# Attention scores on halves of TensorE's rows, and branch outputs split by quarters, in a hybrid decoder layer

## The chip, the core and the metric

The kernel runs on one core of a Trainium2 chip. The metric is the device time of one execution, in microseconds (us); a lower time is better. Before the change the median of three runs is 769.07 us (769.01 to 769.11). In the profile PE is TensorE (PEld its weight loads), DVE is VectorE, ACT is ScalarE, POOL is GpSimd and SP is SyncE.

## The reference, cut to what matters

One layer over 512 tokens of width 1024, in float32. Three branches of attention read the same normalized input: a sliding-window one (8 query heads and 2 key heads of 64, band of two blocks of 128 keys), a stick-breaking one (8 heads of 64) and one over a memory of 256 tokens. Their outputs go through one matrix each, are gated and summed; then come an output matrix, a norm, and a SwiGLU feed-forward.

```
u = rms_norm(h, ln_mix_pre[l])
proj = jnp.einsum('bsd,de->bse', u, w_in[l])
qa, ka, va, qb, kb, vb, qm, gl = jnp.split(proj, split_idx, axis=-1)
# sliding window, per head of 64 and block of 128 queries
scores = jnp.einsum('bnqhgd,bnkhd->bnhgqk', qb, kband) * (d ** -0.5)
...
# stick-breaking, per head of 64: a[t,s] = beta_ts * prod over s<j<t of (1 - beta_tj)
z = jnp.einsum('bqhd,bkhd->bhqk', q[:, i * BLOCK:L], k[:, :L]) * (d ** -0.5)
...
merged = (g[:, :, 0] * jnp.einsum('bse,ed->bsd', y_swa, w_branch_swa[l])
          + g[:, :, 1] * jnp.einsum('bse,ed->bsd', y_sb, w_branch_sb[l])
          + g[:, :, 2] * jnp.einsum('bse,ed->bsd', y_mem, w_branch_mem[l]))
mix = jnp.einsum('bsd,de->bse', merged, w_out[l])
```

## The kernel before, in words

**Products.** A float32 factor is split into a high part in a short float format (fp32r) and the low part that is left over. `split` (L423) does it: ACT casts the high part, DVE subtracts. `parts` (L548) makes two buffers of it. `mm3` (L455) then multiplies with three matmuls, high by high, high by low, and low by high. Nearly all of PE's stream consists of such threes, with 128 rows of weights and 256 or 512 columns of data. The large products (gates, branch matrices, feed-forward) are made in a form with seven products of quarters p1 to p7 in place of eight.

**Stages.** The head loads the first weights and x, sums the squares of x on PE with a matrix of ones (`rstd_of`, L518; its two matmuls use the high and the low part sh_x and sl_x, and on_x holds the ones), and begins the first three key projections (L1141 to L1209; nine matmuls on a constant run before them). `proj` (L581) makes the projections of queries and keys, transposed: 128 rows are the 64 dimensions of two heads, c = 0 to 3 counts such pairs. Then come the stick-breaking heads, the sliding-window heads and the memory heads, with projections, gates and branch products run between as a stream of weights (`dn.run(us)`), then the output matrix and the feed-forward.

**Scores before.** A head has 64 dimensions, and its three products are put into two matmuls over all 128 rows: `stack_parts` (L553) builds, for each head, a buffer with the high part in one half of the rows and the low part in the other (kbs for stick-breaking keys, qas for sliding-window queries). `stack_twice` (L564) builds a buffer with the high part in both halves (qbs, kas) and one with the low part in one half and zeros in the other (qbl, kal). `sb_head` (L1273) has these two matmuls for each of four blocks of queries (keys 512, 384, 256 and 256 columns wide), and three PSUM banks for a head:

```
mm(out, qs[:, q], keys, r < 3, False)
mm(out, ql[:, q], keys, False, r != 2)
```

Then come two sigmoids for each bank, the mask and a scan along the row, `sb_turn` (L1306) turns the weights by transposes, and `sb_out` (L1323) sums the values for two heads at once, each head on one half of TensorE's columns (at and wide in the profile). `swa_pair` (L1348) has four blocks of 256 keys for each of two heads, two matmuls each, later a softmax, transposes, and weighted sums on halves of the columns (pts and wide).

**Branch outputs before.** `pair_out` (L1265) takes a bank with the outputs of two heads: it splits it from the bank into a high and a low buffer, and `seven_raw` (L892) copies the bank once more, in quarters, from which the sums for p3, p5, p6, p7 are made. p1, p2 and p4 use the split parts directly (`seven_left`, L913).

**Order.** Engines run their instructions in the order in which they were given. Tables of numbers (`ORDER`, one for each engine, L38 to L147) fix that order and `follow` (L480) ties each instruction to the one ahead. `PLAN` (L148 to L179) gives each tile its buffer: eight PSUM banks, four raw, high and low weight buffers, and single and paired buffers of 512 columns (ck, pair). All instructions go through a helper that records them, so that the profile gives line L232 for every one; names of tiles tell them apart.

Of the kernel before, what the change touches and what calls it, by code (L numbers as in the profile page):

```python
# [37 lines left out]
ORDER = {  # L38
    "tensor": (
# [23 lines left out]
    ),  # L63
    "vector": (
# [81 lines left out]
    ),  # L146
}  # L147
PLAN = {  # L148
    "raw": (
# [2042 lines left out]
```

## Time and profile before

| | before |
|---|---|
| median of three runs | 769.07 us |
| span of the profiled execution | 766.9 us |
| PE busy | 759.1 us (99%), 4073 matmuls |
| DVE busy | 675.2 us (88%), 1100 instructions |
| ACT busy | 520.3 us (68%), 946 instructions |
| POOL busy | 104.1 us (14%) |
| last matmul ends, from the span's start | 760.3 us |

The profiled execution's span runs from its first to its last instruction; the median of the runs is 2.2 us above it. Busy times of engines overlap. In the timeline a row has its start, its duration, the engine, the operation, output tile, inputs, and their shapes (`128*128` is the part of TensorE's array that is used: rows by columns); equal instructions in a run stand in one row with their count. The end of a matmul is modelled, and the next starts before it, so starts are compared. In brackets stands how long the engine idled just before, and for what. A group has busy time and the mean of one in ns.

### The profile page before, as it was taken

To read this page: it belongs to the slowest core of one execution; us is meant where nothing else is said; L and a number is where in the kernel's file an instruction comes from. 1 tells how busy PE (TensorE), PEld (TensorE's weight loads), DVE (VectorE), ACT (ScalarE), POOL (GpSimd) and SP (SyncE) were. 2 spreads that over 40 slices of the span, in tenths; PEclk is the share of its full clock that TensorE was granted. 3 is DMA by queue.
4 is the path that set the end of the run, shared out by engine and by line. 5 is a ranking of instruction groups with operands and counts; after the bars stand their busy time and mean duration, and the time that the engine had idled before them with its cause. 6 is when DMAs were issued, how large, how long until landed. Compare 5 with 4: busy or idle time off the path is not lost.

```text
span 766.9 us, 11497 instructions
## 1 busy us (share of the span) xinstructions
PE 759.1 (99%) x4073; PEld 647.3 (84%) x4073; DVE 675.2 (88%) x1100; ACT 520.3 (68%) x946; POOL 104.1 (14%) x140
## 2 busy tenths in 40 slices
PE   9999999999999999999999999999999999999996
PEld 6789888778888888888888899988888888888885
DVE  7994897799989756999897799899999999999966
ACT  7662677777997758677944596566666668957552
POOL 0303242000222110010001201100000000214000
PEclk9999999999999999999999999999999999999998
DMA  8548999734799895469949958876777746859922
GB/s 277 166 142 233 332 328 254 211 111 149 185 188 192 184 203 163 112 134 210 340 128 329 209 130 240 203 191 180 204 192 203 220 142 187 171 120 216 261 75 111
DMA packets 50170, 150.06 MB, mean 196 GB/s; under 512 B 5984, under 2 KB 7952, under 8 KB 50016
## 3 DMA queue, kind: packets, MB, share of 16 engines
q1 hardware_dynamic: 34224, 94.38, 36.8%
q0 software_dynamic: 15600, 54.80, 36.1%
q8 instruction: 32, 0.52, 0.3%
q14 instruction: 26, 0.21, 0.1%
q10 hardware_dynamic: 288, 0.13, 0.1%
HBM read 140.38 MB, written 19.40 MB: 208 GB/s over the span
## 4 chain that ended last, share of the span: by engine, by line
PE 96%; DMA 1%; DVE 1%; ACT 1%; issue 0%; SPq 0%; DVEq 0%
PE bank L232 96%; DMA xT<-in_xT 1%; DMA raw<-in_w_p 0%; DVE xacc L232 0%; SPq L232 0%; ACT pair L232 0%; DVE pair L232 0%; ACT hi L232 0%; ACT xT L232 0%; DVE lo L232 0%; DVE fg L232 0%; DVE sl_x L232 0%; DVEq L2180 0%; DVE s L232 0%; ACT sqr L232 0%
## 5 line engine op out<-in xcount | busy, mean ns | idle before, releaser
L232 PE MATMUL bank<-pair,hi 128*128 128x512 f32 (+1 forms) x1008 | 254.4, 368 | 0.0
L232 DVE TENSOR_TENSOR lo<-raw,hi 128x1024 fp32r<-128x1024 f32 (+4 forms) x149 | 170.7, 1149 | 36.8 <-ACT hi L232 36.2
L232 PEld LDWEIGHTS bank<-pair,hi 128*128 128x128 f32 x1008 | 177.5, 189 | 27.0 <-ACT hi L232 0.9
L232 ACT CAST hi<-raw 128x1024 fp32r<-128x1024 f32 (+4 forms) x149 | 147.7, 998 | 73.7 <-PE bank L232 54.5
L232 PE MATMUL bank<-hi,pair 128*128 128x512 f32 (+1 forms) x628 | 196.3, 374 | 0.0
L232 PE MATMUL bank<-pair,lo 128*128 128x256 f32 (+1 forms) x752 | 154.7, 302 | 0.0
L232 PEld LDWEIGHTS bank<-hi,pair 128*128 128x128 f32 x628 | 115.3, 188 | 19.5 <-issue 0.2
L232 PEld LDWEIGHTS bank<-pair,lo 128*128 128x128 f32 x752 | 115.6, 190 | 10.9 <-DVE lo L232 0.7
L232 PE MATMUL bank<-lo,pair 128*128 128x512 f32 (+1 forms) x330 | 123.6, 375 | 0.0
L232 ACT CAST hi<-wide 128x1024 fp32r<-128x1024 f32 (+1 forms) x61 | 62.2, 1024 | 27.0 <-PE bank L232 11.3
L232 DVE TENSOR_TENSOR lo<-wide,hi 128x1024 fp32r<-128x1024 f32 (+1 forms) x61 | 71.9, 1185 | 4.6 <-ACT hi L232 4.3
L232 PEld LDWEIGHTS bank<-lo,pair 128*128 128x128 f32 x330 | 62.0, 188 | 10.1
L232 POOL DMA_DIRECT2D raw<-in_w_g x24 | 21.1, 878 | 124.4 <-DVE lo L232 106.2
L232 DVE TENSOR_TENSOR gp<-gp,bank 128x512 f32<-128x512 f32 x49 | 33.6, 687 | 4.6 <-PE bank L232 3.7
L232 ACT ACTIVATE sg<-gp 128x256 f32<-128x256 f32 x42 | 17.7, 421 | 23.0 <-DVE gp L232 22.9
L232 POOL DMA_DIRECT2D raw<-in_w_gu x15 | 13.2, 924 | 147.6 <-DMA raw<-in_w_gu 138.5
L232 ACT COPY gp<-bank 128x512 f32<-128x512 f32 x42 | 24.7, 588 | 2.1 <-DVE aq L232 1.4
L232 DVE TENSOR_TENSOR_SCAN bw<-br,bw 128x512 f32<-128x512 f32 (+3 forms) x32 | 24.6, 809 | 0.2
L232 DVE TENSOR_TENSOR gp<-gp,hp 128x512 f32<-128x512 f32 x36 | 24.7, 685 | 0.0
L232 POOL DMA_DIRECT2D wide<-in_w_gu x12 | 11.2, 934 | 84.6 <-DMA wide<-in_w_gu 76.3
L232 ACT COPY hp<-bank 128x512 f32<-128x512 f32 x36 | 21.5, 598 | 0.0
L232 PE MATMUL bank<-hi,ll 128*128 128x512 f32 x50 | 19.4, 389 | 0.0
(624 smaller groups left out, 1371.8 us busy)
## 6 DMA issues: line engine op xcount, KB each, us to landing
wide<-in_w_gu SPq DMA_DIRECT2D x31, 512.0 KB, 5.1
raw<-in_w_gu SPq DMA_DIRECT2D x26, 512.0 KB, 5.4
raw<-in_w_g POOLq DMA_DIRECT2D x24, 512.0 KB, 6.0
raw<-in_w_g SPq DMA_DIRECT2D x18, 512.0 KB, 4.2
raw<-in_w_gu POOLq DMA_DIRECT2D x15, 512.0 KB, 7.2
raw<-in_w_p SPq DMA_DIRECT2D x14, 512.0 KB, 6.3
wide<-in_w_gu POOLq DMA_DIRECT2D x12, 512.0 KB, 5.8
raw<-in_w_brt SPq DMA_DIRECT2D x9, 512.0 KB, 4.8
```

The lines of the kernel that those rows point to most:

```text
L232: ins = f(*args, **kw)
```

## The change

1. Queries and keys of both branches are split by plain `parts` on all 128 rows: one cast and one subtraction of 128x512 for a pair of heads. `stack_parts`, `stack_twice` and the zeroed halves go.
2. Scores come from a new function. It makes the three products on 64 rows, once for rows 0 to 63 (the first head of the pair) and once for rows 64 to 127 (the second head), into different banks, head by head in turn. There are 192 score matmuls in place of 128. Two stick-breaking heads start together and hold six banks; `sb_head` becomes `sb_scores`, `sb_weights` and `sb_turn`, and the loop goes over pairs.

```
-        ks, qs, ql = (st[(x, c, h % 2)] for x in ("kbs", "qbs", "qbl"))
...
-            mm(out, qs[:, q], keys, r < 3, False)
-            mm(out, ql[:, q], keys, False, r != 2)
+    def mm3_rows(outs, l, r, start):
+        for x, y_ in ((0, 0), (1, 0), (0, 1)):
+            for e, out in enumerate(outs):
+                rows = slice(64 * e, 64 * e + 64)
+                mm(out, l[x][rows], r[y_][rows], start and x + y_ == 0, y_ == 1)
+    def sb_scores(c):
+        (kh, kl), (qh, ql) = st[("kbs", c)], st[("qbs", c)]
+        z = [[aps(f"z{2 * c + e}{i}") for i in range(3)] for e in range(2)]
...
+            mm3_rows([z[e][i][:, o : o + n] for e in range(2)], (qh[:, q], ql[:, q]), keys, r < 3)
+        for e in range(2):
+            sb_weights(2 * c + e, z[e])
...
-    for h in range(8):
-        sb_head(h)
...
+    sb_scores(0)
+    dn.run(5.6)
+    for c in range(4):
+        sb_turn(2 * c)
...
+        if c < 3:
+            sb_scores(c + 1)
+        dn.run(3.0)
+        sb_turn(2 * c + 1)
```

3. A branch output leaves its bank once, in the quarters' copies. The quarters that are left factors of p1, p2 and p4 are split from those copies: three splits for a branch, where it was four from the bank.

```
+    YRAW = dict(p1=(0, 0), p2=(1, 0), p4=(1, 1))
...
     def pair_out(b, c, ps):
-        y[(b, c)] = parts(f"y{b}{c}", ps)
-        if b in SEVENS:
-            seven_raw(b, c, ps)
...
+        for p, quarter_of in YRAW.items():
+            if c % 2 == 1 and quarter_of[0] == c // 2:
+                ysum[(b, p)] = parts(f"ys{b}{p}", yq[(b, *quarter_of)])
```

4. Instructions are no longer issued while the program is built. They are noted (`Program`, `Notes`, `View`) and put out at the end in one global order, from which each engine's order follows; unused other paths are dropped. The profile's line becomes L421 (`put_out`). `ORDER` and `PLAN` have new numbers throughout, of which this line tells nothing more than that:

```
+    "2826 2829 2702 2827 2844 2830-2831 2711 2832-2833 2820 2845 3143 2834 2846-2849 2723 2850 2855 2838 2856 "
```

Counted over the program: matmuls 4009 before and 4073 after (the profile's page of before counts 64 more than the program has), ACT casts and copies 581 and 565, ACT table loads 9 and 10 (the new one ahead of the first logarithm), DVE two-tensor operations 761 and 745, DVE copies 20 and 10, POOL's zeroings 17 and 7. A stretch of PE's order in which the array is used in one form (whole, by halves of the columns, by halves of the rows) is followed by one in another form: there are 17 stretches before (8 of them halves of the columns) and 35 after (8 halves of the columns, 13 halves of the rows, 14 whole). Before, each column stretch lies between two stretches of the whole array; after, the order goes directly between row halves and column halves eight times.

In the new order PE's first stick-breaking scores, which stood before as these rows (kbs keys, qbs and pair the two query buffers, hi and lo weights):

```order
L232 MATMUL bank_104<-kbs_316,qbs_409 128x512
L232 MATMUL bank_104<-kbs_316,pair_111 128x512
L232 MATMUL bank_104<-kbs_316,qbs_409 128x384
L232 MATMUL bank_104<-kbs_316,pair_111 128x384
L232 MATMUL bank_104<-kbs_316,qbs_409 128x256
L232 MATMUL bank_104<-kbs_316,pair_111 128x256
```

now stand as these (a last letter h or l is the high or the low part, x2 the two halves of the rows):

```order
L421 MATMUL bank_101<-kbs0h,qbs0h 128x384 x2
L421 MATMUL bank_101<-kbs0h,qbs0l 128x384 x2
L421 MATMUL bank_101<-kbs0l,qbs0h 128x384 x2
L421 MATMUL bank_101<-kbs0h,qbs0h 128x512 x2
L421 MATMUL bank_101<-kbs0h,qbs0l 128x512 x2
L421 MATMUL bank_101<-kbs0l,qbs0h 128x512 x2
L421 MATMUL bank_101<-kbs0h,qbs0h 128x256 x2
```

Every block of queries has three such pairs for two heads, in place of two matmuls for each head.

On PE the two matmuls of the sum of squares stood next to each other (they are the rows with on_x):

```order
L232 MATMUL bank_104<-pair_109,lo_82 128x512
L232 MATMUL bank_104<-sh_x,on_x 128x512
L232 MATMUL bank_104<-sl_x,on_x 128x512
L232 MATMUL bank_104<-pair_111,hi_79 128x512
L232 MATMUL bank_104<-pair_114,hi_79 128x512
```

Now, with pair_102 the ones and pair_112 and pair_113 the high and the low part of the sum, they are apart:

```order
L421 MATMUL bank_101<-pair_112,pair_102 128x512
L421 MATMUL bank_101<-pair_104,hi_79 128x512
L421 MATMUL bank_101<-pair_105,hi_79 128x512
L421 MATMUL bank_101<-pair_104,lo_83 128x512
L421 MATMUL bank_101<-pair_105,hi_79 128x512
L421 MATMUL bank_101<-pair_106,hi_79 128x512
L421 MATMUL bank_101<-pair_105,lo_83 128x512
L421 MATMUL bank_101<-pair_106,hi_79 128x512
L421 MATMUL bank_101<-pair_113,pair_102 128x512
```

Seven matmuls of the fourth projection have moved between them.

At the head of DVE's order stood these (pair and wide are the first block of u and of x, lo_80 the low part of the first weight):

```order
L232 CAST on_x<-const-bfloat16-1.0 128x128
L232 CAST on_m<-const-bfloat16-1.0 128x128
L232 MEMSET none 1x512
L232 MEMSET eps_t 128x1
L232 TENSOR_SCALAR pair_111<-wide_84 128x256
L232 SCALAR_TENSOR_TENSOR pair_114<-wide_84,pair_111 128x512
L232 TENSOR_TENSOR lo_80<-raw_72,hi_76 128x128
```

Now they stand so (pair_102 is on_x, the first pair_104 takes the place of on_m):

```order
L421 CAST pair_102<-const-bfloat16-1.0 128x128
L421 TENSOR_TENSOR lo_80<-raw_72,hi_76 128x128
L421 CAST pair_104<-const-bfloat16-1.0 128x128
L421 TENSOR_SCALAR pair_104<-wide_84 128x256
L421 MEMSET eps_t 128x1
L421 SCALAR_TENSOR_TENSOR pair_105<-wide_84,pair_104 128x512
```

The low part of the first weight and a cast of ones have moved ahead of the first block of u.

More of the change, by code (lines that the diff above doesn't have):

```diff
@@ L1 @@
 import math
-from contextlib import ExitStack, nullcontext
+from contextlib import ExitStack
 import numpy as np
@@ new lines, with __init__, then, __getitem__ @@
+class View:
+    def __init__(self, make, path=(), shape=None):
+        self.make, self.path, self.shape = make, path, shape
+    def then(self, f):
+        return View(self.make, self.path + (f,))
+    def __getitem__(self, k):
+        return self.then(lambda ap: ap[k])
+    def bitcast(self, dt):
+        return self.then(lambda ap: ap.bitcast(dt))
+    def rearrange(self, *args, **kw):
+        return self.then(lambda ap: ap.rearrange(*args, **kw))
+    def unsqueeze(self, axis):
+        return self.then(lambda ap: ap.unsqueeze(axis))
+    def to_broadcast(self, shape):
+        return self.then(lambda ap: ap.to_broadcast(shape))
+    def real(self):
+        ap = self.make()
+        for f in self.path:
+            ap = f(ap)
+        return ap
@@ new lines, with __init__, put_out @@
+class Op:
+    def __init__(self, at, engine, name, args, kw):
+        self.at, self.engine, self.name, self.args, self.kw = at, engine, name, args, kw
+        self.behind = ()
+class Program:
+    def __init__(self):
+        self.ops = []
+    def put_out(self, nc, order, follow):
+        real = lambda x: x.real() if isinstance(x, View) else x
+        last, out = {}, set()
+        for n in order or range(len(self.ops)):
+            op = self.ops[n]
+            assert all(b.at in out for b in op.behind)
+            out.add(n)
+            args = [real(x) for x in op.args]
+            ins = getattr(getattr(nc, op.engine), op.name)(*args, **{k: real(x) for k, x in op.kw.items()})
+            if op.engine in last:
+                follow(ins, last[op.engine])
+            last[op.engine] = ins
+        assert len(out) == len(self.ops)
@@ L256, in __getitem__, with once, f @@
         return self.held[c]
+def once(make):
+    got = []
+    def f():
+        if not got:
+            got.append(make())
+        return got[0]
+    return f
 class Places:
@@ L268, in open, with fixed, take @@
     def open(self, pool, kind, n, shape, dt=F32):
[L269 removed]
+        for i in range(n):
             key = f"{kind}{i}"
             self.held[key] = pool.tile(shape, dt, tag=key, name=key, bufs=1)
[L273 to L277 removed]
+    def fixed(self, shape, name):
         if name == "v_all":
             self.spare = self.used
[L280 to L287 removed]
+        t = self.held["wide0"][:, self.used : self.used + shape[1]]
+        self.used += shape[1]
+        return t
+    def take(self, pool, kind, shape, dt, name):
         n = int(next(self.plan[kind]))
         if kind == "ck" and n < SINGLES:
[L290 removed]
+            return View(once(lambda: pool.tile(shape, dt, tag=f"ck{n}", name=name, bufs=1)))
         if kind == "ck":
+            assert dt == F32R
             n -= SINGLES
@@ L380, in tile_kernel @@
 def tile_kernel(ctx, tc, a):
-    nc = Core(tc.nc)
+    program = Program()
+    nc = Core(program)
     places = Places()
@@ L425, in split @@
         ins = nc.scalar.copy(hi, raw)
-        lows = nc.vector.tensor_tensor(lo, raw, hi.bitcast(F32), op=ALU.subtract)
-        if "behind" in st:
-            after(ins, st["behind"][0])
-            after(lows, st["behind"][1])
+        nc.vector.tensor_tensor(lo, raw, hi.bitcast(F32), op=ALU.subtract)
         return ins
@@ L441, in w_split @@
         uid[0] += 1
-        hi = places.take(wp, "hi", [P, 1024], F32R, f"hi{uid[0]}", bufs=4)
-        lo = places.take(wp, "lo", [P, 1024], F32R, f"lo{uid[0]}", bufs=4)
+        hi = places.take(wp, "hi", [P, 1024], F32R, f"hi{uid[0]}")
+        lo = places.take(wp, "lo", [P, 1024], F32R, f"lo{uid[0]}")
         if isinstance(raw, list):
             for i, x in enumerate(raw):
-                ins = split(x[:, :], hi[:, i * 512 : (i + 1) * 512], lo[:, i * 512 : (i + 1) * 512])
+                split(x[:, :], hi[:, i * 512 : (i + 1) * 512], lo[:, i * 512 : (i + 1) * 512])
         else:
-            ins = split(raw[:, :n], hi[:, :n], lo[:, :n])
-        if "chain" in st:
-            after(ins, st["chain"])
+            split(raw[:, :n], hi[:, :n], lo[:, :n])
         return hi, lo
@@ L456, in mm3 @@
         (lh, ll), (rh, rl) = l, r
-        one = nc.tensor.matmul(out, lh, rh, start=start, stop=False, skip_group_check=True)
+        nc.tensor.matmul(out, lh, rh, start=start, stop=False, skip_group_check=True)
         nc.tensor.matmul(out, lh, rl, start=False, stop=False, skip_group_check=True)
-        return one, nc.tensor.matmul(out, ll, rh, start=False, stop=stop, skip_group_check=True)
-    def mm3_behind(*args):
-        one, last = mm3(*args)
-        if "products" in st:
-            after(one, st["products"])
-        st["products"] = last
+        nc.tensor.matmul(out, ll, rh, start=False, stop=stop, skip_group_check=True)
     def mm(out, l, r, start, stop):
@@ L474, in tile_kernel @@
     pin, since = [], []
-    def after(ins, first):
-        if not ORDER:
-            follow(ins, first)
     def follow(ins, first):
@@ L486, in fn @@
         ins = nc.scalar.activation(*args, **kw)
-        for p in pin:
-            after(ins, p)
+        ins.behind = tuple(pin)
         since.append(ins)
@@ L494, in table, with const @@
         ins = nc.scalar.preload_act_table_set(name)
-        for x in since:
-            after(ins, x)
+        ins.behind = tuple(since)
         since.clear()
         pin[:] = [ins]
-    def const(name, shape, pool=cst):
-        t = places.fixed(cst, shape, F32, f"c_{name}") if pool is cst else pool.tile(shape, F32, name=f"c_{name}")
+    def const(name, shape, pool=None):
+        t = pool.tile(shape, F32, name=f"c_{name}") if pool else places.fixed(shape, f"c_{name}")
         nc.sync.dma_start(t[:, :], a[name])
@@ L1210, in tile_kernel @@
-    pin[:] = [first_table]
+    idle = tc.nc.const_aps.tensor(1.0, [P, 512], BF16)
+    one_t = {}
+    for name in ("x", "m"):
+        one_t[name] = ck(f"on_{name}", F32R)[:, :P]
+        nc.vector.tensor_copy(one_t[name], idle[:, :P])
+    pw = dps("warm")
+    for i in range(WARM):
+        mm(pw[:, :], idle[:, :P], idle[:, :], True, True)
+    first_load(nc.scalar, 0, (0, 2))
+    first_table = nc.scalar.preload_act_table_set("natural_log_exp_and_others")
+    pin[:] = [first_table]
+    load_x(0, 1)
@@ new lines, in tile_kernel @@
+    first_load(nc.sync, 0, (1,))
+    load_x(1, 2)
+    first_load(nc.sync, 1, (0, 1))
+    load_x(2, 3)
+    first_load(nc.sync, 1, (2,))
+    first_load(nc.sync, 2, (0,))
+    load_x(3, 4)
+    first_load(nc.sync, 2, (1, 2))
+    load_x(4, 5)
+    first_load(nc.sync, 3)
+    load_x(5, 8)
+    dn.loaded = dn.have = FIRST
+    for p in range(len(PIECE)):
+        for i in range(FIRST):
+            first_split(i, p)
+        for k in range(*PIECE[p]):
+            gain_split(k)
+    xacc = ck("xacc")
@@ new lines, in tile_kernel @@
+    nc.scalar.activation(xacc[:, :], xraw[0][:, :], AF.Square)
+    for k in range(1, KC):
+        nc.scalar.activation(xraw[k][:, :], xraw[k][:, :], AF.Square)
+        nc.vector.tensor_tensor(xacc[:, :], xacc[:, :], xraw[k][:, :], op=ALU.add)
+    dn.ahead(4, 3)
+    for i in range(FIRST):
+        first_ps[("kb", i)] = aps(f"kb{i}")
+    order = [(i, 0, x) for x in ("hh", "lh", "hl") for i in range(FIRST)]
+    order += [(i, 1, x) for i in range(FIRST) for x in ("hh", "lh", "hl")]
+    for i, k, x in order:
+        w = (his if x[0] == "h" else los)[i]
+        mm(first_ps[("kb", i)][:, :], w[:, k * P : (k + 1) * P], u[k][x[1] == "l"], k == 0 and x == "hh", False)
@@ L1212, in tile_kernel @@
+    gens = [dn.units[i]["mm"](his[i], los[i]) for i in range(FIRST)]
+    for k in range(2, KC + 1):
+        for g in gens:
+            next(g, None)
+    dn.at = FIRST
+    st["rs"], st["rb"] = rstd_of("x", xacc, S, aps)
+    for f in st.pop("waiting"):
+        f()
     ident = const("ident", [P, P], base)
-    sinks = places.fixed(cst, [P, 8], F32, "sinks")
+    sinks = places.fixed([P, 8], "sinks")
     nc.sync.dma_start(sinks[:, :], a["sinks"].to_broadcast([P, 8]))
@@ L1620, in turn @@
         st[("t1", t)] = t1
-        return place("T1", t, t1)
+        place("T1", t, t1)
     def kept(t):
@@ L2065, in tile_kernel @@
     kept(1)
-    behind(since[-1], st["mixed"])
     table("silu_and_others")
@@ L2071, in tile_kernel @@
     go(3)
-    behind(*turn(3, tmp[3]))
+    turn(3, tmp[3])
     fs.hold = 5
@@ L2075, in tile_kernel @@
     turn_n2(2)
-    behind(*turn_n2(3))
+    turn_n2(3)
     fs.hold = 6
@@ L2079, in tile_kernel @@
     turn_n22(2)
-    behind(*turn_n22(3))
+    turn_n22(3)
     fs.hold = 8
@@ L2089, in tile_kernel @@
         turn_late(t, 1)
-    st.pop("behind")
     fs.hold = 10**6
@@ L2094, in tile_kernel @@
     go(len(fs.units))
-    for e, text in ORDER.items():
-        seen, last = getattr(nc, e).seen, None
-        for part in text.split():
-            a, _, b = part.partition("-")
-            for k in range(int(a), int(b or a) + 1):
-                if last is not None:
-                    follow(seen[k], seen[last])
-                last = k
+    order = []
+    for part in ORDER.split():
+        a, _, b = part.partition("-")
+        order += range(int(a), int(b or a) + 1)
+    program.put_out(tc.nc, order, follow)
 def _buckets():
```

411 lines of the change are left out of this document (118 added, 293 removed), and 421 rows, old and new, of tables (ORDER, PLAN).

## The prediction

> **What bounds the kernel now.** I began with the page's head and its table of busy time.
>
> ```profile
> span 766.9 us, 11497 instructions
> PE 759.1 (99%) x4073; PEld 647.3 (84%) x4073; DVE 675.2 (88%) x1100; ACT 520.3 (68%) x946; POOL 104.1 (14%) x140
> ```
>
> TensorE (PE) is busy for 99% of the span, VectorE (DVE) for 88%. A busy PE may still be waiting inside, so the waits of PE came next, and the chain that ended last.
>
> ```profile
> PE bank L232 <- PEq L2174: 0.8, 1, 0.8
> PE bank L232 <- DVE sl_x L232: 0.4, 1, 0.4
> ```
>
> ```profile
> 22.29 737.97 PE bank L232 x3990
> ```
>
> PE waits twice: 0.8 us at the start, and 0.4 us for one low part (sl_x). From 22.29 us the chain is PE alone, 3990 matmuls to 760.3 us. The table by stretches gives the two ends (first column the stretch, then its length, busy time of PE, PEld, DVE, ACT, POOL; granted clock third from the end).
>
> ```profile
> 4.75:80.00 75.25, 74.88 (x396) 66.10 (x396) 61.40 (x100) 44.09 (x73) 15.59 (x29) 1.00 0.69 210
> ...
> 760.30:766.93 6.63, 0.00 (x0) 0.00 (x0) 2.46 (x6) 1.17 (x4) 0.00 (x0) 0.68 0.43 158
> ```
>
> The clock is full from the first real matmul, so a gain or a loss will have to be a change in PE's stream: matmul time, gaps at a change of form, waits. The last 6.6 us (final sums, output) follow PE's end, and the change leaves their work as it is: 0.
>
> Work taken off DVE and ACT is worth nothing by itself. The groups show what such work is: the halves of heads were split by instructions like this one.
>
> ```profile
> L232 DVE TENSOR_TENSOR kbs<-kb,kbs 64x512 fp32r<-64x512 f32 x5 | 3.4, 685 | 0.1
> L232 ACT ACT_TABLE_LOAD x9 | 11.5, 1283 | 1.8 <-PEq L2174 1.7
> ```
>
> DVE issues 16 subtractions fewer, about 16 x 0.685 = 11 us, and 10 small copies. But PE waited for DVE 0.4 us in all, so at most that could come back, and it is counted below in its place. ACT gets a table load more, 1.28 us, ahead of the first logarithm; the projections that fill the banks meanwhile cover it, and if that cover is gone it costs 1.28 us.
>
> **1. The scores.** In the timeline of the first stick-breaking head (start, duration; a row's end is modelled, so I count from start to start):
>
> ```profile
> 81.53 0.40 PE L232 MATMUL bank<-kbs,qbs 128*128 128x512 f32 x1
> 81.76 0.39 PE L232 MATMUL bank<-kbs,pair 128*128 128x512 f32 x1
> 81.99 0.33 PE L232 MATMUL bank<-kbs,qbs 128*128 128x384 f32 x1
> 82.16 0.34 PE L232 MATMUL bank<-kbs,pair 128*128 128x384 f32 x1
> 82.33 0.28 PE L232 MATMUL bank<-kbs,qbs 128*128 128x256 f32 x1
> 82.45 0.28 PE L232 MATMUL bank<-kbs,pair 128*128 128x256 f32 x1
> ...
> 82.82 0.40 PE L232 MATMUL bank<-pair,hi 128*128 128x512 f32 x1
> ```
>
> A matmul starts 0.23, 0.17 or 0.12 us after the one ahead of it (512, 384, 256 columns). A head takes 82.82 - 81.53 = 1.29 us, eight heads 10.3. A sliding-window head is eight matmuls of 256, 8 x 0.12 = 0.96, eight heads 7.7. Together 18.0 us for 128 matmuls.
>
> After it there are 192, in 96 pairs: each product once on rows 0 to 63 and once on rows 64 to 127, for the two heads of a pair, into two banks. If the two overlap fully, a pair costs what one of them does: stick-breaking 3 products x (0.23 + 0.17 + 0.12 + 0.12) = 1.92 us for two heads, four times, 7.7; sliding window 12 x 0.12 = 1.44, four times, 5.8. Together 13.5, a gain of 4.5. If nothing overlaps, 27.0, a loss of 9.0. No row of before has halves of the rows, so this is the number that decides. The nearest rows are halves of the columns, in the weighted sums that follow the scores:
>
> ```profile
> 108.85 0.28 PE L232 MATMUL bank<-kbs,qbl 128*128 128x256 f32 x1
> 109.05 2.38 PE L232 MATMUL bank<-at,wide 128*64 128x512 f32 x16
> 111.36 0.39 PE L232 MATMUL bank<-mh,hi 128*128 128x256 f32 x1
> 111.58 0.28 PE L232 MATMUL bank<-ml,hi 128*128 128x256 f32 x1
> ```
>
> ```profile
> 175.40 1.73 PE L232 MATMUL bank<-pts,wide 128*64 128x256 f32 x16
> 177.06 0.39 PE L232 MATMUL bank<-pair,qas 128*128 128x256 f32 x1
> 177.28 0.28 PE L232 MATMUL bank<-kal,qas 128*128 128x256 f32 x1
> ```
>
> Each block's 16 rows are 8 pairs of halves, in the first block 512, 384, 256 and 128 columns wide, twice each, in the second 256, 256, 256 and 128, twice each: 20 and 14 pairs of 128 columns. They took 111.36 - 109.05 = 2.31 and 177.06 - 175.40 = 1.66 us. From the two, such a pair costs (2.31 - 1.66) / 6 = 0.108 us and the constant is 0.14. One matmul of 128 columns on the whole array is hardly cheaper: transposes, 128 columns each, run at
>
> ```profile
> 89.64 1.25 PE L232 MATMUL bank<-c_ident,bw 128*128 128x128 f32 x10
> 90.65 0.48 PE L232 MATMUL bank<-kbs,qbs 128*128 128x512 f32 x1
> ```
>
> (90.65 - 89.64) / 10 = 0.10 us. So column halves do run side by side at the price of one. I take the same for row halves: **-4.5 us**. If the 256-wide pairs came at 0.109 rather than 0.12, it would be 72 x 0.011 = 0.8 to 1.1 more.
>
> **2. Changes of form.** Around the column block: 0.20 us from the last score to the first half (0.12 would be the pace), 0.14 inside as the constant, and 0.22 from 111.36 to 111.58 (again 0.12). That is 0.08 + 0.14 + 0.10 = 0.32 us for one excursion out of the whole array and back, 0.16 a switch. By the order of the program, PE has 17 stretches of one form before, so 16 switches, and 35 after, so 34: 18 more, **+2.9 us**. Of these five are excursions more; the other eight go from row halves to column halves directly. If such a direct change were free it would be 5 x 0.32 = +1.6. If each of the 13 row blocks had to show 0.05 us of its first load besides, +3.6.
>
> The Trainium skill, "TensorEngine Tiling (Array Packing)", section Tiling Modes, says that changing the mode (and not only the tile) drains TensorE, which speaks against this change. The trace agrees, with its 0.32 us for an excursion, and by it the change costs 2.9 of the 4.5 us that it gains.
>
> **3. The wait for sl_x.** In the timeline:
>
> ```profile
> 21.54 0.39 PE L232 MATMUL bank<-sh_x,on_x 128*128 128x512 f32 x1
> 22.29 0.50 PE L232 MATMUL bank<-sl_x,on_x 128*128 128x512 f32 x1 [0.37 <-DVE sl_x L232]
> 22.64 0.64 PE L232 MATMUL bank<-pair,hi 128*128 128x512 f32 x2
> ```
>
> From the first sum to the second it takes 0.75 us, not 0.23, and to the next matmul 0.35, not 0.23: 0.64 lost. In the new order seven projection matmuls (7 x 0.23 = 1.6 us) stand between the two sums, so DVE's 0.68 us for sl_x are covered: **-0.64** (0 if DVE comes to it later: it has a small load-dependent subtraction ahead of it now).
>
> **4. The head.** What holds the first real matmul:
>
> ```profile
> 0.74 3.44 DMA raw<-in_w_p
> ```
>
> (from the chain: the first piece of a weight), and in the timeline:
>
> ```profile
> 0.92 0.48 DVE L232 CAST on_m<-const-bfloat16-1.0 128x128 fp32r<-128x128 bf16 x1
> 4.00 0.35 DVE L232 TENSOR_SCALAR pair<-wide 128x256 fp32r<-128x256 f32 x1 [2.05 <-DMA wide<-in_xg]
> 4.41 0.68 ACT L232 CAST hi<-raw 128x128 fp32r<-128x128 f32 x3
> 4.75 1.02 PE L232 MATMUL bank<-pair,hi 128*128 128x512 f32 x3
> 5.21 0.69 DVE L232 TENSOR_TENSOR lo<-raw,hi 128x128 fp32r<-128x128 f32 x3
> 5.61 0.92 PE L232 MATMUL bank<-pair,lo 128*128 128x512 f32 x3
> ```
>
> In the new order DVE has the first weight's low part, which needs its high part and so the piece landed at 0.74 + 3.44 = 4.18, and then the cast of on_m, ahead of the first half of x. On DVE's queue: 4.18 + 0.23 (one of ACT's three casts) + 0.23 (one of three subtractions) + 0.48 + 0.35 = 5.47 us, and PE's first real matmul waits for it: 0.7 later than 4.75. Part of that comes back, since PE ran slowly there anyhow, 5.61 - 4.75 = 0.86 us for three matmuls that need 0.68. I take **+0.5** (0 if the rest of the head absorbs it all, since the chain is PE's own only from 22.29 us on; +0.7 if nothing does).
>
> **5. New waits.** The tables give other buffers and another order everywhere. PE stops once in 738 us now. I take one such stop more, **+0.4**, with 0 below. Above stands the case in which a pair's scores find no free bank and PE waits for a head's six sigmoids:
>
> ```profile
> L232 ACT ACTIVATE br<-bank 128x384 f32<-128x384 f32 x16 | 8.2, 514 | 0.2 <-PE bank L232 0.2
> L232 ACT ACTIVATE bw<-bank 128x384 f32<-128x384 f32 x16 | 7.6, 537 | 0.0
> L232 ACT ACTIVATE br<-bank 128x512 f32<-128x512 f32 x8 | 4.9, 614 | 0.5 <-PE bank L232 0.5
> ```
>
> 2 x 0.51 + 2 x 0.54 + 2 x 0.61 = 3.3 us once.
>
> **Sum.** -4.5 + 2.9 - 0.64 + 0.5 + 0.4 = -1.3 us. The profiled execution's span is 766.9, so 765.6 after; the median of the runs is 2.2 above the span, and the same difference gives 769.07 - 1.3 = 767.7 us. About 0.2% (1.5 us) is what a measurement of this kernel can tell from no change, so "faster" begins at 767.5 and "slower" at 770.6. The forecast lies beside the first of these.
>
> **The rivals.**
>
> *The halves share something in part (slower).* If a pair must take in two loads of 128 columns one after the other, at the transposes' pace of about 0.11 us each, a 256-wide pair costs 0.22 and not 0.12 and a 384-wide one 0.22 and not 0.17; a 512-wide one stays. 72 x 0.10 + 12 x 0.05 = +7.8 us, so 767.7 + 7.8 = 775.5. It decides from the point where a 256-wide pair costs 0.12 + 1.3 / 72 = 0.14 us, where the whole gain is gone. Against it: column halves load 64 columns each, two loads a pair, and show none of it; but their loads are half as big. Chance 0.06. Half-way, 0.17 a pair, it is +3.9 and 771.6 us, chance 0.05.
>
> The Trainium skill, "TensorE: Matmul & The Clock Gate", Part 3, on packing by rows and columns, has a measured 3.07 times for four row tiles where 4 would be full. Scaled to two tiles that is an estimate of 1.54 times, 27.0 / 1.54 = 17.5 us for the scores and hence 771.7 us; no run here shows it yet, and the trace's column halves speak against it.
>
> *The halves do not overlap at all.* +9.0 in place of -4.5, 767.7 + 13.5 = 781.2. For it speaks only that nothing here shows row halves; chance 0.05.
>
> *Banks.* A pair of stick-breaking heads now holds six of eight banks where a head held three. Queued behind the waiting matmul on PE is everything. One stop of 3.3 us in the place of the 0.4 gives 770.6, two give 773.9. Against it: between the first two blocks of scores stand 51 matmuls, 51 x 0.23 = 11.7 us, more than the 6.6 us of both heads' sigmoids. Chance 0.13.
>
> *The change does not do what it says:* the order lists the pairs as described, so this has no chance of its own; it would be the case without overlap.
>
> **How the numbers follow.** My forecast, with full overlap, has 0.71; its own range is 766.0 to 770.0 (-5.6 in step 1 and +1.6 in step 2 on the one side, +3.6, +0.7 and a stop or two on the other). Its point is 767.7. For 8 in 10 I take 765.8 to 772.0, which adds the half-way case and one stop for banks, and leaves out the dearer cases, about 0.16, and a little below. Faster by over 0.2%: somewhat over half of the forecast, 0.38. Same: 0.33 of the forecast and 0.05 of the banks, 0.38. Slower: 0.08 + 0.06 + 0.05 + 0.05 = 0.24.
>
> **What would show it.** In the changed kernel's timeline a stick-breaking block of 24 row-half matmuls should last 1.9 us and about 0.3 for its switches; 2.9 with two loads a pair, 4.2 with no overlap. PE's waits should have no row for sl_x; the first real matmul should start near 5.5 us; DVE's busy time should fall by over 11 us without effect. I am wrong if PE's waits hold a row of several us for a bank, or if the scores' pairs start further apart than 0.14 us.

## The result, and the profile after

The changed kernel took 780.62 us (median of 4 runs, 778.01 to 782.19), the kernel before 769.04 (768.66 to 769.11): a ratio of 1.015, 95% interval 1.0128 to 1.0172. It is slower by 11.6 us, beyond the whole range of the prediction. The profiled execution took 782.19 us, which is at the upper end of the runs, with a span of 780.4, 13.5 above the span before. Sums over one trace below stand against the 13.5, comparisons of kernels use medians.

The head of the page and the table of busy time of the changed kernel:

```profile
span 780.4 us, 11609 instructions
PE 766.3 (98%) x4137; PEld 638.2 (82%) x4137; DVE 658.5 (84%) x1074; ACT 507.2 (65%) x931; POOL 100.5 (13%) x130
```

DVE lost 16.7 us of work and ACT 13.1, and PE's share fell by one per cent. The waits of PE (total, times, longest):

```profile
PE bank L421 <- ACT gq1p L421: 2.4, 1, 2.4
PE bank L421 <- ACT gq2p L421: 0.9, 2, 0.6
PE bank L421 <- PEq L2251: 0.8, 1, 0.8
PE bank L421 <- ACT gq0p L421: 0.8, 1, 0.8
PE bank L421 <- ACT hi L421: 0.6, 2, 0.3
...
PE bank L421 <- DVE lo L421: 0.5, 1, 0.5
```

Before there were two such rows. sl_x is gone, and most of the new names (gq0p, gq1p, gq2p, lo) belong to the gates and their weights in the middle of the kernel. The chain that ended last (start, length) says what those waited for:

```profile
7.42 201.77 PE bank L421 x1185
...
224.26 6.12 DMA xq<-xq
230.66 9.00 DMA xq<-xq
240.21 0.59 ACT gq1p L421
...
246.76 10.11 DMA raw<-in_w_g
...
477.14 293.24 PE bank L421 x1578
```

Before, the chain was PE alone from 22.29 us on. Now it leaves PE after 209 us, and transfers stand in it: sums of the gates' input x in DRAM (xq) and loads of the gates' weights (in_w_g). The timelines of ACT and PE around 240 us show one such place in full. First ACT:

```profile
239.69 0.62 ACT L421 CAST pair<-xq 128x512 fp32r<-128x512 f32 x1 [2.64 <-DMA xq<-xq]
240.21 0.58 ACT L421 COPY gq1p<-bank 128x512 f32<-128x512 f32 x1
```

and PE:

```profile
238.02 0.39 PE L421 MATMUL bank<-lo,pair 128*128 128x512 f32 x1
240.84 0.50 PE L421 MATMUL bank<-hi,pair 128*128 128x512 f32 x1 [2.44 <-ACT gq1p L421]
```

The transfer issued at 230.66 landed 9.00 us later, at 239.66. ACT's cast waited for it, the copy that empties a bank stood behind the cast on ACT's queue, and PE waited for the bank. The row names gq1p, but the cause is the transfer.

The stretch from 226 to 440 us of before and then of after (length, busy time of PE, PEld, DVE, ACT, POOL; granted clock, DMA share, GB/s):

```profile
226.00:440.00 214.00, 214.00 (x1016) 178.68 (x1016) 178.40 (x280) 145.81 (x264) 26.36 (x30) 1.00 0.79 199
```

```profile
226.00:440.00 214.00, 208.03 (x962) 166.82 (x963) 177.10 (x270) 144.99 (x256) 34.52 (x41) 1.00 0.90 233
```

The DMA engines are busier there (0.90 for 0.79), and between 80 and 226 us idler (0.68 for 0.77). What moved is on POOL's queue: the sums of branch weights in DRAM (ws0p, ws2p), 512 KB a transfer. Before:

```profile
63.47 1.15 POOL L232 DMA_DIRECT2D ws0p<-in_w_brt  x2
64.61 1.02 POOL L232 DMA_DIRECT2D ws2p<-in_w_brt  x2
...
142.93 0.82 POOL L232 DMA_DIRECT2D ws1p<-in_w_brt  x1 [7.12 <-DMA ws1p<-ws1p]
192.05 0.92 POOL L232 DMA_DIRECT2D xq<-xq  x1 [48.30 <-ACT xq L232]
```

After:

```profile
122.41 0.58 POOL L421 DMA_DIRECT2D ws0p<-in_w_brt  x1
175.99 0.95 POOL L421 DMA_DIRECT2D xq<-xq  x1 [52.99 <-DVE yq L421]
176.59 1.22 POOL L421 DMA_DIRECT2D ws0p<-in_w_brt  x1
...
205.15 0.99 POOL L421 DMA_DIRECT2D ws0p<-in_w_brt  x1 [5.58 <-DMA ws0p<-ws0p]
...
231.71 0.88 POOL L421 DMA_DIRECT2D xq<-xq  x1 [0.17 <-issue]
...
234.45 0.89 POOL L421 DMA_DIRECT2D ws2p<-in_w_brt  x1
...
287.70 0.84 POOL L421 DMA_DIRECT2D ws2p<-in_w_brt  x1 [1.17 <-DMA ws2p<-ws2p]
```

All sums of weights were issued between 63 and 143 us, ahead of the gates. Now those of the stick-breaking branch (ws0p), but for the first, stand between the sums of x, and those of the memory branch (ws2p) among the loads of the gates' weights. POOL was idle for 53 us in between.

What the change is named after went as forecast. The timeline of the first pair of heads:

```profile
81.57 0.28 PE L421 MATMUL bank<-sl_m,pair 128*128 128x256 f32 x1
81.78 0.45 PE L421 MATMUL bank<-kbs0h,qbs0h 64*128 64x384 f32 x2
82.06 0.34 PE L421 MATMUL bank<-kbs0h,qbs0l 64*128 64x384 f32 x2
82.23 0.34 PE L421 MATMUL bank<-kbs0l,qbs0h 64*128 64x384 f32 x2
82.41 0.40 PE L421 MATMUL bank<-kbs0h,qbs0h 64*128 64x512 f32 x2
...
83.91 0.50 PE L421 MATMUL bank<-pair,hi 128*128 128x512 f32 x1
```

Each row is two matmuls on the two halves. From one pair to the next are 0.17 and 0.23 us, the pace of one matmul, and the 24 matmuls last 83.91 - 81.78 = 2.13 us.

Counted over the whole of both traces (start to start of matmuls, beyond the pace of each form), the 13.5 us are: scores -4.5; changes of form +4.0; gaps and waits elsewhere +13.8, of which 10.7 lie between 220 and 420 us; the rest, 0.2, is behind PE's last matmul.

### The profile page after: what moved, and what is told of

It reads as the page before. It is cut to its first block, busy times and chain, and to the rows that moved or that the text cites. A ratio compares the mean times of both kernels' runs of the same rounds, so it can differ in the third digit from the quotient of the medians.

```text
span 780.4 us, 11609 instructions
## 1 busy us (share of the span) xinstructions
PE 766.3 (98%) x4137; PEld 638.2 (82%) x4137; DVE 658.5 (84%) x1074; ACT 507.2 (65%) x931; POOL 100.5 (13%) x130
## 4 chain that ended last, share of the span: by engine, by line
PE 87%; DMA 6%; DVE 2%; ACT 2%; issue 2%; POOL 0%; SPq 0%; DVEq 0%; ACTq 0%; POOLq 0%
PE bank L421 87%; DMA raw<-in_w_g 2%; DMA xq<-xq 2%; DMA raw<-in_w_brt 1%; DVE lo L421 1%; ACT hi L421 1%; DVE fg L421 0%; DVE s L421 0%; DMA raw<-in_w_p 0%; ACT gq2p L421 0%; ACT pair L421 0%; POOL xq L421 0%; DVE sy L421 0%; SPq L421 0%; ACT wide L421 0%
## 5 line engine op out<-in xcount | busy, mean ns | idle before, releaser
L421 PE MATMUL bank<-pair,hi 128*128 128x512 f32 (+1 forms) x1064 | 270.1, 366 | 0.3 <-ACT hi L421 0.3
L421 PE MATMUL bank<-hi,pair 128*128 128x512 f32 (+1 forms) x844 | 254.8, 381 | 4.9 <-ACT gq1p L421 2.4
L421 ACT CAST hi<-raw 128x1024 fp32r<-128x1024 f32 (+4 forms) x151 | 149.7, 998 | 102.0 <-PE bank L421 70.0
L421 PEld LDWEIGHTS bank<-pair,hi 128*128 128x128 f32 x1064 | 184.4, 189 | 30.7 <-ACT hi L421 1.4
L421 DVE TENSOR_TENSOR lo<-raw,hi 128x1024 fp32r<-128x1024 f32 (+4 forms) x151 | 172.2, 1149 | 37.7 <-ACT hi L421 30.3
L421 PEld LDWEIGHTS bank<-hi,pair 128*128 128x128 f32 x844 | 155.3, 188 | 38.3 <-ACT gq1p L421 3.2
L421 PE MATMUL bank<-pair,lo 128*128 128x256 f32 (+1 forms) x784 | 167.0, 302 | 0.0
L421 PE MATMUL bank<-lo,pair 128*128 128x512 f32 (+1 forms) x418 | 153.6, 379 | 0.5 <-DVE lo L421 0.5
L421 PEld LDWEIGHTS bank<-pair,lo 128*128 128x128 f32 x784 | 124.2, 189 | 10.9
L421 PEld LDWEIGHTS bank<-lo,pair 128*128 128x128 f32 x418 | 78.2, 188 | 14.6 <-DVE lo L421 1.5
L421 ACT CAST hi<-wide 128x1024 fp32r<-128x1024 f32 (+1 forms) x59 | 60.6, 1028 | 44.4 <-PE bank L421 22.1
L421 DVE TENSOR_TENSOR lo<-wide,hi 128x1024 fp32r<-128x1024 f32 (+1 forms) x59 | 69.6, 1184 | 6.1 <-ACT hi L421 3.5
L421 DVE TENSOR_TENSOR gp<-gp,bank 128x512 f32<-128x512 f32 x49 | 32.9, 682 | 3.4 <-PE bank L421 2.9
L421 POOL DMA_DIRECT2D raw<-in_w_g x24 | 21.1, 881 | 112.6 <-DVE lo L421 57.0
L421 POOL DMA_DIRECT2D wide<-in_w_gu x15 | 13.1, 875 | 155.4 <-DMA wide<-in_w_gu 126.7
L421 PE MATMUL bank<-pair,mgh 128*128 128x512 f32 x90 | 29.9, 393 | 0.0
L421 ACT COPY gp<-bank 128x512 f32<-128x512 f32 x42 | 24.6, 594 | 5.8 <-PE bank L421 5.8
L421 ACT ACTIVATE sg<-gp 128x256 f32<-128x256 f32 x42 | 17.7, 428 | 14.7 <-DVE gp L421 14.6
L421 DVE TENSOR_TENSOR_SCAN bw<-br,bw 128x384 f32<-128x384 f32 (+3 forms) x32 | 25.3, 814 | 0.3 <-ACT br L421 0.2
L421 DVE TENSOR_TENSOR gp<-gp,hp 128x512 f32<-128x512 f32 x36 | 24.3, 685 | 1.5 <-ACT gp L421 0.7
L421 ACT COPY hp<-bank 128x512 f32<-128x512 f32 x36 | 21.4, 598 | 4.1 <-PE bank L421 4.1
L421 POOL DMA_DIRECT2D raw<-in_w_gu x12 | 10.5, 875 | 84.7 <-DMA raw<-in_w_gu 83.9
```

What stands on the lines that cost most here:

```text
L421: ins = getattr(getattr(nc, op.engine), op.name)(*args, **{k: real(x) for k, x in op.kw.items()})
```

## The experiments

My theory was that the sums of weights, late on POOL's queue, crowd the gates' transfers, and so PE. The rivals: the row halves cost more than their pace shows; or the new order of PE, DVE and ACT is dearer by itself. "Before" in each is the kernel before on the same chip, 768.61 to 768.72 us.

**Sums late in the kernel before.** In POOL's order the sums of ws0p and ws2p go where the changed kernel has them, and nothing else moves. The first two lines of the order (41 to 48 are ws0p's, 49 to 56 ws2p's):

```diff
-"4-11 20 35-36 3 0-1 15-18 14 19 2 41 43 49 51 42 44 50 52 21 26 45 33 12 31 53 25 24 23 22 27 29 28 34 30 13 "
-"32 46 54 37 47 55 38 48 56 39-40 57 61 58-59 65 64 60 62 66 63 67-88 91 93 90 94 92 89 96 95 97-121 130-135 "
+"4-11 20 35-36 3 0-1 15-18 14 19 2 21 26 33 12 31 25 24 23 22 27 29 28 34 30 13 "
+"32 37 38 39-40 41 43 57 42 44-46 61 58-59 47 65 64 48 60 62 66 63 67-69 49 70-72 50-51 73 53 74 52 54 75-77 55 78-80 56 81-88 91 93 90 94 92 89 96 95 97-121 130-135 "
```

> The kernel before with the opposite edit: the same sixteen transfers moved to where the change put them, ws0p around the first sum of x and ws2p among the gate weights on POOL's queue. Nothing else differs from the kernel before. Theory 1: waits like those of the changed kernel appear in the gate stage, 773 to 780 us. Theories 2 and 3: 768.5 to 770.

Measured: 781.96 us (1.0172, 1.0157 to 1.0188), +13.3. The waits of PE:

```profile
PE bank L232 <- ACT hi L232: 3.1, 1, 3.1
PE bank L232 <- ACT gq1p L232: 2.8, 1, 2.8
```

The place of 16 transfers alone costs the kernel before as much as the whole change, and row halves are not needed for such a loss. The equal size is in part chance. At the waits of 3.1 and 2.8 us the granted clock (a share of full speed) fell to 0.50 for 6.8 and 3.4 us, and matmuls of 512 columns then started 0.43 us apart instead of 0.23: by an estimate from these stretches, about 4 of the 13 us. In the changed kernel the clock stays full over the same stage (1.00 above), so it has no such part.

Then each chain alone, first ws0p's (41 to 48 moved as above, 49 to 56 left):

```diff
-"4-11 20 35-36 3 0-1 15-18 14 19 2 41 43 49 51 42 44 50 52 21 26 45 33 12 31 53 25 24 23 22 27 29 28 34 30 13 "
+"4-11 20 35-36 3 0-1 15-18 14 19 2 49 51 50 52 21 26 33 12 31 53 25 24 23 22 27 29 28 34 30 13 "
```

> The kernel before with only the stick-breaking branch's eight transfers moved to where the change put them, around the first sums of x on POOL's queue. If the hold-up of POOL's queue ahead of the sums of x is what costs: most of the 13.3 us of e4, 776 to 781 us. If it is the DMA engines' load among the gate weights: 770 to 774.

Measured: 778.29 us (1.0124, 1.0107 to 1.014), +9.7. In its trace POOL issues the last four sums of x from 224 to 234 us (before, from 211 to 223), after it has waited 4.9 us for a sum of ws0p that stands ahead of them on its queue; DVE waits 5.4 us for a sum of x, and PE 3.9 us for DVE. About 4 us are again a clock of 0.50 after the waits. And ws2p's alone:

```diff
-"4-11 20 35-36 3 0-1 15-18 14 19 2 41 43 49 51 42 44 50 52 21 26 45 33 12 31 53 25 24 23 22 27 29 28 34 30 13 "
+"4-11 20 35-36 3 0-1 15-18 14 19 2 41 43 42 44 21 26 45 33 12 31 25 24 23 22 27 29 28 34 30 13 "
```

> The kernel before with only the memory branch's eight transfers moved to where the change put them, among the gate weights on POOL's queue. If the load among the gate weights is what costs: 775 to 780 us. If the hold-up ahead of the sums of x is: 769 to 772.

Measured: 772.19 us (1.0045, 1.003 to 1.006), +3.6. The two add up: 9.7 + 3.6 = 13.3. So most of it hangs on the eight transfers that hold up the sums of x, and less on the eight among the gates' weights.

**Sums early in the changed kernel.** The reverse edit: the numbers are instructions of the program, and those in a list go behind the one beside it.

```diff
+MOVES = [([1072, 1089, 1073, 1090, 1119], 817), ([1120, 1198, 1199], 190)]
...
+    for ops, at in MOVES:
+        for n in ops:
+            order.remove(n)
+        k = order.index(at) + 1
+        order[k:k] = ops
```

This one moves ws2p's, to 61 to 122 us:

> The changed kernel with only the memory branch's eight transfers (ws2p) moved to where they stood before. Theory 1: the waits between 225 and 240 us stay, those from 250 to 300 us shrink: 774 to 778 us. Theories 2 and 3: 778 to 782.

Measured: 777.46 us (1.0112, 1.0097 to 1.0127), 3.2 less than the changed kernel. No wait on gq1p beyond 0.2 us was left. With ws0p's moved instead:

```diff
+MOVES = [([862, 892, 863, 893, 997], 817), ([998, 1027, 1028], 190)]
```

> The changed kernel with only the stick-breaking branch's eight transfers (ws0p) moved to where they stood before. Theory 1: the sums of x (xq) come some 10 us earlier and the three waits of 2.6, 0.6 and 0.7 us between 225 and 240 us go, the later ones stay: 775 to 778 us. Theories 2 and 3: 778 to 782.

Measured: 778.76 us (1.014, 1.012 to 1.016), 1.9 less. That is not clear of the noise, since the interval overlaps that of the changed kernel (1.0128 to 1.0172), and it lies in the rivals' range. With both:

```diff
+MOVES = [([862, 1072, 892, 1089, 863, 1073, 893, 1090, 997, 1119], 817), ([998, 1120, 1027, 1198, 1028, 1199], 190)]
```

> The changed kernel with one edit: the sixteen transfers on POOL's queue that add up the branch weights of the stick-breaking and of the memory branch (ws0p, ws2p) stand where they stood before the change (issued from about 61 to 115 us), not among the gates (176 to 208 and 234 to 300 us). Theory 1, the sums crowd the gate stage (they hold POOL's queue ahead of the sums of x, and the DMA engines while gate weights are needed): PE's time beyond the matmuls' pace between 220 and 420 us, 12.5 us in the changed kernel, falls to 2 to 4, and the time to 769 to 772 us. Theory 2, the new order and buffers of the gate stage itself are late, wherever the sums stand: 778 to 782. Theory 3, the changes of TensorE's form cost more than I took: nothing changes here, 778 to 782.

Measured: 787.25 us (1.0244, 1.0227 to 1.0261), 6.6 more. The longest wait of PE, and the stretch in which it lies:

```profile
PE bank L422 <- DVE mk L422: 7.2, 1, 7.2
```

```profile
100.00:120.00 20.00, 12.75 (x70) 10.22 (x71) 13.79 (x24) 7.80 (x14) 5.45 (x8) 0.83 0.92 230
```

The gates' stage was relieved by about half (gaps between 220 and 420 us fell from 12.5 to 6.8 us, not to the 2 to 4 that I expected), but rows_v and vnext, for which DVE is ready at 97 us, now landed late behind the sums (vnext at 105 us). So I tried the stretch from 122 us, where POOL is idle:

```diff
+MOVES = [([862, 1072, 892, 1089, 863, 1073, 893, 1090, 997, 1119, 998, 1120, 1027, 1198, 1028, 1199], 616)]
```

> The changed kernel with the sixteen transfers of the two branches' sums placed right behind the reads of the bias (about 122 us), in front of the first sum of x, where POOL's queue stood idle until 176 us. Theory 1 (sums crowd whatever stage they stand in): neither the wait of 7.4 us for mk of the first experiment nor the waits between 225 and 300 us; PE's time beyond its pace between 220 and 420 us about 6 us, 774 to 777 us. Theory 2 (the first experiment was slow for another reason): a wait of several us elsewhere, 778 or more.

Measured: 786.75 us (1.0234, 1.0219 to 1.0249), a miss. The wait of PE, and in ACT's timeline what is behind it:

```profile
PE bank L422 <- ACT at L422: 4.8, 1, 4.8
```

```profile
150.34 1.04 ACT L422 CAST hi<-raw 128x1024 fp32r<-128x1024 f32 x1 [8.67 <-DMA raw<-in_w_brt]
```

A branch weight, loaded just in time, was late in its turn. One chain in each free stretch (ws2p's at 61 us, seven of ws0p's at 122):

```diff
+MOVES = [([1072, 1089, 1073, 1090, 1119], 817), ([1120, 1198, 1199], 190), ([892, 863, 893, 997, 998, 1027, 1028], 862)]
```

> The changed kernel with the two chains of sums apart from each other: the memory branch's where they stood before (61 to 115 us, as in e3), the stick-breaking branch's eight right behind the first of them at 122 us. Half as many at once as in e5. Theory 1 (what counts is how many transfers stand at once where weights are awaited): no wait over 1 us before 320 us, 773 to 777 us. Rival (any move of the first chain into 120 to 170 us makes ACT wait for a weight, as in e5): a wait of 3 to 5 us near 146 us, 780 to 786.

Measured: 781.65 us (1.0166, 1.0151 to 1.0182), not less than the changed kernel and in the rival's range, with waits of 1.8 us for the same bank at 146 us and 1.9 for gq2p at 365. Nowhere that I tried did the new order have room for both chains. Why the kernel before has room for them between 63 and 143 us is not settled.

**The loads of w_out.** They come earlier than before too, among the last gates' weights. Nine of them moved back, on top of the sums at 122 us:

```diff
+MOVES = [([862, 1072, 892, 1089, 863, 1073, 893, 1090, 997, 1119, 998, 1120, 1027, 1198, 1028, 1199], 616), ([3097, 2908, 2909], 2985), ([3024, 3023, 2981], 3027), ([2982, 3142, 3143], 3006)]
```

> The kernel of e5 with nine of the sixteen loads of w_out moved behind the last gate loads (issued about 360 us, not 319 to 345; before the change all sixteen stood at 360 to 378). Theory 1, extended: the waits for copies of the third branch's gate banks (gq2p) between 340 and 400 us, some 4 us, fall to 1 or 2, and the time is 2 to 3 us under that of e5: 771 to 774 us. Rival (ACT's order there, with casts of w_out among the gates, is at fault, not the transfers): as e5.

Measured: 785.59 us (1.0223, 1.0208 to 1.0239), 1.2 less than without that edit: inconclusive, since the two intervals overlap. A wait of 2.3 us on gq2p remained; ahead of that bank's copies ACT waited 2.3 us for a branch weight. A cleaner way, with the memory branch's sums early: w_out's loads read 32 of 512 columns, repeated by the casts; the other columns are left out.

```diff
-            nc.sync.dma_start(t[:, :], a["w_out"][:, h, k])
+            nc.sync.dma_start(t[:, :32], a["w_out"][:, h, k, :32])
```

> The kernel of e3 with the same order of instructions, but each load of w_out reads only 32 of its 512 columns, repeated by the splits that follow; the other columns of w_out are left out. If w_out's transfers crowd the third branch's gate weights: the excess of PE between 320 and 400 us, 4.3 us in e3, falls to 1 to 2, and the time 2 to 4 us under e3's 777.5. If the order of ACT's work there is at fault: 777 to 778 as e3.

Measured: 774.89 us (1.0082, 1.0065 to 1.0099), 2.6 less than with full loads, and no row for gq2p is left. These transfers are a second part of the crowding.

**The halves.** Are they side by side because neighbours in the order go to different halves? Here all three products of one half stand ahead of the three of the other (on top of the sums at 122 us, 786.75):

```diff
-        for x, y_ in ((0, 0), (1, 0), (0, 1)):
-            for e, out in enumerate(outs):
-                rows = slice(64 * e, 64 * e + 64)
+        for e, out in enumerate(outs):
+            rows = slice(64 * e, 64 * e + 64)
+            for x, y_ in ((0, 0), (1, 0), (0, 1)):
```

> The kernel of e5 with the two loops of the score function exchanged: three products on rows 0 to 63, then three on rows 64 to 127, so that only every third matmul has a neighbour on the other half. If halves of the rows run side by side only when neighbours in the order: four slots for six matmuls and not three, 13.5 us of scores becoming 18, the time 4 to 5 us over e5. If they did so at any distance, or if the time of a score were not that of its slot: as e5.

Measured: 785.16 us (1.021, 1.0193 to 1.0227), not slower. The first block's start and the matmul after it:

```profile
83.13 0.45 PE L422 MATMUL bank<-kbs0h,qbs0h 64*128 64x384 f32 x2
...
85.27 0.73 PE L422 MATMUL bank<-pair,hi 128*128 128x512 f32 x2
```

2.14 us, as before the edit. A half does not wait for three of the other half that stand ahead of it.

**A change of form by itself.** In the kernel before, two whole-array matmuls that follow a block of column halves go into it, behind its first and its third group; 16 excursions more:

```diff
-530-537 613-620
+530-531 613 532-535 614 536-537 615-620
```

> The kernel before, with in each of its eight blocks of scores on column halves the two whole-array matmuls that follow the block put between its pairs (after the first and after the third): 16 excursions into and out of the halves more, no other change to order, buffers or transfers. By the price of an excursion in step 2 of the prediction (0.32 us) 16 x 0.32 = 5.1 us more than the kernel before: about 774; at 0.39 us, as a block on row halves costs in the profile of the changed kernel, 775. If changes of form are free, or lie beside other work, 768.5 to 769.5.

Measured: 774.5 us (1.0075, 1.0061 to 1.0088), +5.9, 0.37 for an excursion. The first of the eight blocks:

```profile
109.05 1.08 PE L210 MATMUL bank<-at,wide 128*64 128x512 f32 x4
110.06 0.38 PE L210 MATMUL bank<-mh,hi 128*128 128x256 f32 x1
110.37 1.30 PE L210 MATMUL bank<-at,wide 128*64 128x384 f32 x8
```

The single matmul of 256 columns takes 110.37 - 110.06 = 0.31 us in place of 0.12.

**Transfers made light in both kernels.** Some 5 of the 13.5 us were still without a cause. Every streamed weight up to the feed-forward (and its sums in DRAM, and w_out) is cut to 32 columns, which the casts repeat; instructions and order stay.

```diff
-        nc.sync.dma_start(raw[:, :n], src)
+        nc.sync.dma_start(raw[:, :32], src[:, :32])
...
-        nc.gpsimd.dma_start(t[:, :], src, accum_op=ALU.add)
+        nc.gpsimd.dma_start(t[:, :32], src[:, :32], accum_op=ALU.add)
```

> The kernel before with every streamed weight transfer up to the feed-forward (projections, branch weights, gates, their sums in DRAM, w_out) cut to 32 of its columns, which the casts and subtractions repeat; the other columns are left out. PE waits for nothing of weight in the kernel before, so both theories expect its own time within 1 us: 768 to 769.5.

> The changed kernel with the same cut (32 columns of each streamed weight up to the feed-forward; the rest left out): order, buffers and instructions are those of the changed kernel, and transfers cost almost nothing. Theory (all of the loss beyond the forecast's terms comes from transfers that land late): the excess of 10.7 us between 220 and 420 us is gone; against the lightened kernel before -4.5 for the scores, +4.0 for changes of form, +2 for small gaps in the feed-forward, whose transfers stay: +1.5, so 769.5 to 771.5. Rival (the new order itself, by buffers or by the queues of DVE and ACT, holds PE up, some 5 us that moving the sums and cutting w_out did not bring back): 774 to 777.

Measured: before 768.65 us (1.0001, 0.9991 to 1.001), after 774.12 (1.007, 1.0055 to 1.0085). The head of the light changed kernel, and its two longest waits behind the start:

```profile
span 772.2 us, 11607 instructions
```

```profile
PE bank L421 <- ACT pair L421: 0.5, 1, 0.5
PE bank L421 <- ACT hi L421: 0.3, 1, 0.3
```

Transfers cost the kernel before nothing, and the changed one 780.62 - 774.12 = 6.5 us by medians, 780.4 - 772.2 = 8.2 in the spans. But 774.12 - 768.65 = 5.5 us stay; 774.12 lies in the rival's 774 to 777 and above the theory's 769.5 to 771.5. My theory is right for about half of the loss: 6.5 of 11.6 us by medians (the changed kernel's runs differ among themselves by 4 us, so the share is rough). For the other half the rival stands: the new order of PE, DVE and ACT, with its buffers, is dearer by itself. (The sums of x and the feed-forward's transfers stayed whole in both light kernels, so these are not excluded for a part of it.) The spans of the two light kernels differ by 772.2 - 766.6 = 5.6: scores -4.5, changes of form +4.0, behind the last matmul +0.2, and +5.8 of gaps elsewhere. Of these 0.9 are in the first 40 us, 1.1 are five waits of 0.17 to 0.32 us between 230 and 470 us, and 3.8 are gaps under 0.15 us, spread from 40 to 660 us.

In the feed-forward most such gaps stand before a matmul that waits for nothing. But the matmul ahead of the gap often does wait, too shortly for the table. One such place in the light changed kernel (PEld is the load of weights):

```profile
526.48 0.59 ACT L421 COPY hp<-bank 128x512 f32<-128x512 f32 x1
...
527.12 0.19 PEld L421 LDWEIGHTS bank<-pair,hi 128*128 128x128 f32 x1
527.12 0.50 PE L421 MATMUL bank<-pair,hi 128*128 128x512 f32 x1
...
527.46 0.52 PE L421 MATMUL bank<-pair,lo 128*128 128x256 f32 x3
```

ACT's copy frees a bank at 526.48 + 0.59 = 527.07 us. The load of weights that waited for it starts 0.05 later, together with its matmul, and the next matmul comes 0.34 us after that one, not 0.23. Counted over 40 to 660 us, 35 gaps of 0.03 to 0.15 us (2.8 us) follow a matmul whose load started within 0.06 us of what it waited for, 19 times ACT and 16 times DVE; in the light kernel before there are 8 (0.7 us). So some 2.1 of the 3.8 us are operands and banks that DVE and ACT deliver just in time. What makes the rest is open.

## Why the prediction was wrong, point by point

**1. The scores: right.** -4.48 us by the paces in the trace, for -4.5. Both rivals without full overlap are refuted, by the 0.17 and 0.23 us from pair to pair.

**2. Changes of form: right in kind, too low.** +4.0 us for +2.9, above the bound of +3.6: 6.9 us in all for 2.9 before. In the light kernel 21 blocks of halves cost 0.33 us each. A block of rows alone costs 0.39 (0.09 to enter, 0.19 inside, 0.11 to leave), and where rows follow columns directly it costs 0.18 inside in three places and 0.31 to 0.37 in the other three: a direct change is free only in part. So scores and changes of form together bring -0.5 us, not -1.6.

The Trainium skill, "TensorEngine Tiling (Array Packing)", section Tiling Modes, says that a change of mode drains TensorE; the 0.37 us for an excursion agrees.

**3. The wait for sl_x: right**, and **4. the head: right in sign.** The timeline of the changed kernel at both places:

```profile
5.05 0.93 PE L421 MATMUL bank<-pair,hi 128*128 128x512 f32 x3 [0.29 <-ACT hi L421]
...
22.19 0.39 PE L421 MATMUL bank<-pair,pair 128*128 128x512 f32 x1
22.42 0.63 PE L421 MATMUL bank<-pair,hi 128*128 128x512 f32 x2
```

The second sum stands in the plain pace. The first real matmul starts 0.30 us later than before, not 0.7. The step had DVE's queue decide this start; the row names ACT's cast of the weight, so its reason is not confirmed, and the right sign is in part luck.

**5. New waits: the step that failed.** The prediction said that the tables give "other buffers and another order everywhere" and priced that at one stop, +0.4, with 3.3 us for a bank above it. It measured +13.8 with the sl_x wait and the head in it. The step looked for a wait among PE, DVE and ACT, and had no term for the transfers on the queues of POOL and SP, though the sums' 16 transfers of 512 KB move there by up to 234.45 - 64.61 = 170 us. The profile before gave a hint: the DMA share over the gates' stage was already 0.79, and the sums raised it to 0.90. The rival of the banks was a wait of this size at the wrong place: the banks of the scores cause none of PE's waits; banks of the gates do, because ACT's queue stands still for a transfer.

The light kernels say what remains when the streamed weights cost almost no transfer: slower by 5.5 us, and 774.12 is still beyond 772.0. The prediction took the order of PE, DVE and ACT to cost nothing but named waits; in the light kernels it costs 5.8 us, mostly in gaps too short for the table of waits.

No kernel here beat the one before.

## What to carry to other kernels

When an order is redrawn, read the order of the transfers too, on every queue that issues them: list what each large transfer now stands among, and look at the DMA share of that stage. A wait put down to an engine's copy may be a transfer that the instruction ahead of the copy waits for. Where a saving is paid for with changes of form, price them on both sides first: here 4.5 us bought 0.5.

## What the runs showed of the hardware

**Halves of the rows** run fully side by side, 96 pairs at the price of one matmul each, also when three of one half stand ahead of three of the other. The Trainium skill, "TensorE: Matmul & The Clock Gate", Part 3, has 3.07 times for four row tiles; for two halves these runs show the full 2 times.

**A wait of PE can lower the clock.** The stretch with the 4.8 us, of the kernel with the sums at 122 us:

```profile
140.00:160.00 20.00, 15.20 (x68) 11.45 (x68) 9.14 (x15) 6.01 (x10) 2.70 (x4) 0.83 0.94 252
```

The granted clock is 0.83 here on average, as around the 7.2 us above. With the 2.4 us of the changed kernel it stayed at 1.00. But the length of one wait does not decide: in the kernel with the two chains apart the clock fell to 0.50 for 3.4 us after the wait of 1.8 us, and again after the one of 1.9 us:

```profile
367.70:371.10 3.40, 3.40 (x9) 2.62 (x10) 3.13 (x5) 2.57 (x5) 0.00 (x0) 0.50 0.69 233
```

Matmuls of 512 columns start 0.43 us apart there, not 0.23. The Trainium skill, "TensorE: Matmul & The Clock Gate", Part 1, says that the clock falls after an idle window of about 3.4 us. The 4.8, the 7.2 and the 2.4 us agree; the 1.8 and 1.9 us do not, since they are about half of such a window. Why these lowered the clock and the 2.4 us did not, no run here shows.

**Transfers:** the gates' weights that POOL issues landed in 7.9 us after (median) and 6.0 before, those that SP issues in 6.9 and 4.2.
